# Fourfold row copies of a hybrid decoder step: from TensorE matmuls and repeated transposes to transfers through DRAM

## Chip, cores and metric

The kernel runs on one core of one Trainium2 chip. The metric is the device time of one launch in microseconds (us). The kernel before took 2336.71 us (median of 3 runs, 2336.39 to 2338.29). The profiled execution, from which all durations are read, took 2337.24 us; its instructions span 2335.5 us, so 1.7 us lie around the span.

## What is computed

One layer of a hybrid decoder is applied to a prompt of 256 tokens and to a sample group of 8 sequences with 8 new tokens each, 320 token columns in all. Cut to what matters here:

```python
# mLSTM, 4 heads, dk 256, dv 512 (per sequence)
C_new = decay * C + sum_s w_end[s] * k[s] (x) v[s]      # 8 sample states of 256 x 512 per head
# HGRN2, 8 heads, dk 128, dv 256
S_new = exp(G_end) * S + sum_s (k[s] * exp(G_end - G[s])) (x) i[s]   # 8 sample states of 128 x 256 per head
# around them: x @ w_in, sigmoid merge of two branch projections, w_out, LayerNorm,
# relu(x1 @ w_up)^2 @ w_down, LayerNorm
```

The change touches how the outer products for the sample's states get their operands. Each sequence has only 8 tokens, and the products must keep float32 accuracy although the matmuls run in a reduced format (float32r). Every operand is therefore split into a rounded part "hi" and a rest "lo", and a product is hi·hi + hi·lo + lo·hi (+ lo·lo). With a sequence's 8 tokens repeated four times on 32 partitions, keys as (hi, lo, hi, lo) and values as (hi, hi, lo, lo), one matmul over 32 partitions sums all four products at once.

## The kernel before

**Main stream.** The weights are cut into 304 tiles of 2048 rows x 128 columns, each in two units of 1024 rows. A unit is loaded into one of three raw buffers (`wr`), rounded by ACT to `hi` (line 467) and subtracted by DVE to `lo` (line 469); as soon as a raw buffer is free, its next load is issued on SP's queue (`reload`, line 476). `run_main` (line 480) then issues, for each of 16 steps of a tile, three matmuls of 128x320 (lines 504 to 506): 4864 steps and 14592 main matmuls in all. Everything else is side work that is woven in between.

**Who sets the order.** All engines run a fixed order that a planner (`Sched`, line 133) writes down while the kernel is built. Side work is written as generators that ask for an engine with a cost (`("pe", 400, ...)`), wait for events (`wait`), or take and give back a buffer (`acq`, `rel`). The planner keeps a planned clock per engine and issues a side instruction when its planned ready time has come: 140 ns are added from engine to engine (`LAT`) and 450 ns more before TensorE (`PE_LAT`). A DMA is taken to occupy SP for 620 ns, and a fixed allowance is added for its landing (2500 to 4500 ns, by the place in the code). The chip then runs each engine's instructions in that order. Where the allowance is too short, the instruction that needs the data waits in its engine's order, and all that stands behind it on that engine waits too.

**mLSTM heads** (about 87 us each; lines 776 to 1181). `m_V` transposes the values (`PE_T`, line 887), splits them (lines 890, 891), and for the sample multiplies the split rows `vs` by a 0/1 matrix `spread` (line 900, two matmuls of 128x512) to get the fourfold copies `vst`, which ACT evicts (line 901). `m_KW` weights the keys, and for each of two column halves `stack` (line 905) writes the fourfold split keys side by side in a staging tile; four transposes (line 960) turn them, and ACT evicts them to `kst` (line 963). `m_update` (line 1159) runs four matmuls over 32 partitions, four times a head, DVE adds the old state, and `m_store` sends it to DRAM. It waits for the events `KS` and `vst` (line 1162). `m_states` loads the old states, 16 of 256 KB a head.

**HGRN2 heads** (about 50 us each; lines 1184 to 1543). `h_i` transposes and splits the values and spreads them with two matmuls of 128x256 (line 1365) and an eviction (line 1366); `h_state` stacks the keys (line 1404), makes two transposes (line 1406) and an eviction (line 1408). `h_update` (line 1434) runs eight matmuls over 32 partitions once both are there.

**Afterwards** only the main stream is left: merge projections, output projection, the feed-forward part, and the prompt's states at the very end.

Of the kernel before, what the change touches and what calls it, by code (L numbers as in the profile page):

```python
# [8 lines left out]
F32 = mybir.dt.float32  # L9
# [67 lines left out]
def constants():  # L77
    c = np.zeros((128, C_END), np.float32)
    i = np.arange(128)
    c[:, C_ID:C_ID + 128] = i[:, None] == i[None, :]  # L80
    c[:, C_TRI:C_TRI + 128] = i[:, None] <= i[None, :]

    s = np.arange(64)
    t = s.reshape(2, 4, 8).transpose(1, 0, 2).reshape(64)
    c[64:, C_BM:C_BM + 64] = (s[:, None] <= t[None, :]) & (s[:, None] // 8 == t[None, :] // 8)
    for r in range(4):
        c[r, C_SEL + r] = c[r + 8, C_SEL + r] = 1.0
        c[r + 4, C_SEL + 4 + r] = c[r + 12, C_SEL + 4 + r] = 1.0
    start = np.zeros(TOK, bool)
    start[0] = True  # L90
    start[NP_::NT] = True
    c[:4, C_SC:C_SC + TOK] = ~start
    c[:4, C_SC + TOK:C_SC + 2 * TOK] = np.where(start, -1e38, 0.0)
    m = np.zeros((128, len(LEVELS), 64), np.int32)
    for n, b in enumerate(LEVELS):
        right = (i // b) % 2 == 1
        t = i[right]
        m[:, n, :] = (i[:, None] // (2 * b) == t[None, :] // (2 * b)) & ((i[:, None] // b) % 2 == 0)

    r = np.zeros((2, 64, 2, 4, 4, 8), np.float32)  # L100
    for b in range(NB):
        for n in range(4):
            for i in range(8):
                r[1 - n // 2, 8 * b + i, b // 4, b % 4, n, i] = 1.0
    return c, m.reshape(128, -1), r.reshape(128, 256)

# [144 lines left out]
def pe_r(n):  # L251
    return max(108.0, n * 0.425)
# [31 lines left out]
class Program:  # L284
# [48 lines left out]
    def carve(self):  # L333
# [20 lines left out]
        self.bc = Pool([B(712) for _ in range(2)])  # L354
        self.eb0 = B(512)
        self.eb = Pool([self.eb0])
        self.stg = Pool([B(256) for _ in range(2)])
        self.qn0 = B(256)
        self.qn = Pool([self.qn0])
        X = Part(self.rx)  # L360
# [17 lines left out]
        self.ktk = Pool([A.three(2, 128)])  # L378
        self.it2 = [B.three(3, 256) for _ in range(2)]
        self.it = Pool(self.it2)  # L380
        self.hstg = Pool([B(256) for _ in range(2)])
# [19 lines left out]
    def carve_h(self):  # L401
        C = self.Part(self.pool.tile([128, 5120], F32, name="f3h", tag="f3"))
        qz = C(256)
        self.hqz = Pool([qz])
        pp = C(512)
        self.pp = Pool([pp])
        for x in (qz, self.ats0, pp[:, 480:512], *(y[64:128, 2, :] for y in self.it2)):
# [181 lines left out]
    def start(self):  # L589
# [25 lines left out]
        self.dma(self.f2[:, 448:704], d["spread"])  # L615
        self.spread = self.ra[:, 6400:6656].rearrange("p (g n) -> p g n", g=2)
        nc.gpsimd.tensor_copy(self.lmask, lm)
        nc.gpsimd.tensor_copy(self.spread, self.f2[:, 448:704].rearrange("p (g n) -> p g n", g=2))
# [254 lines left out]
    def m_V(self, h):  # L873
# [18 lines left out]
            yield rel(self.sbank, b)  # L892
        yield rel(self.vr, vr)
        yield post(m["Vt"])

        vst = yield acq(self.vst)
        m["vst_"] = vst
        for g in range(2):
            b = yield acq(self.sbank)
            yield ("pe", pe_r(512), lambda: self.mm(b, self.spread[:, g, :], vs, start=True, stop=True))  # L900
            yield ("act", act(512, True), lambda: self.A(vst[:, g, :], b))
            yield rel(self.sbank, b)
        yield post(m["vst"])

    def stack(self, st, src, his):

        v = self.nc.vector
        w = st.rearrange("p (b r t) -> p b r t", r=4, t=8)
        x = src.rearrange("p (b t) -> p b t", t=8).unsqueeze(2).to_broadcast([128, 8, 2, 8])
        step = his[1] - his[0]  # L910
        los = [r for r in range(4) if r not in his]
        pick = lambda rs: w[:, :, rs[0]:rs[0] + 2 * step - (step - 1):step, :]
        hi, lo = pick(his), pick(los)
        yield ("act", act(128), lambda: self.A(hi.bitcast(F32R), x))
        yield ("dve", dve(128), lambda: v.tensor_tensor(lo.bitcast(F32R), x, hi, ALU.subtract))

    def m_KW(self, h):
        nc, v, m = self.nc, self.nc.vector, self.mh[h]
# [33 lines left out]
        kst = yield acq(self.kst)  # L952
        m["kst_"] = kst
        b = yield acq(self.sbank)
        bv = b.rearrange("p (g k) -> p g k", g=2)
        for c in range(2):
            st = yield acq(self.stg)
            yield from self.stack(st, kw[:, c, 256:320], (0, 2))
            for g in range(2):
                yield ("pe", PE_T, lambda: nc.tensor.transpose(bv[:, g, 128 * c:128 * c + 128], st[:, 128 * g:128 * g + 128], self.ident))  # L960
            yield rel(self.stg, st)
        yield rel(self.kw, kw)
        yield ("act", act(512, True), lambda: self.A(kst, bv))
        yield rel(self.sbank, b)
        yield post(m["KS"])

    def ln_post(self, h, i, src, den, hb, parts, psum):

# [215 lines left out]
    def h_start(self, h):  # L1184
# [5 lines left out]
        for n in ("f", "q", "lv", "o", "pre8", "suf", "I", "SP", "S", "aT", "qz", "ist", "sdone", "got", "ld"):  # L1190
            m[n] = Ev()
        m["i"] = [Ev(), Ev()]
        m["Y"] = [Ev() for _ in range(9)]
# [142 lines left out]
    def h_i(self, h):  # L1336
# [25 lines left out]
        b = yield acq(self.sbank)  # L1362
        bv = b.rearrange("p (g k) -> p g k", g=2)
        for g in range(2):
            yield ("pe", pe_r(256), lambda: self.mm(bv[:, g, :], self.spread[:, g, :], vst[:, 0, :], start=True, stop=True))
        yield ("act", act(512, True), lambda: self.A(vst, bv))
        yield rel(self.sbank, b)
        yield post(m["ist"])

    def h_load(self, h):  # L1370

# [13 lines left out]
    def h_state(self, h):  # L1385
# [13 lines left out]
        ks = fs[:, 0, 256:320]  # L1399
        yield ("dve", dve(64), lambda: v.tensor_tensor(ks, qk[:, 0, 256:320], ks, ALU.mult))  # L1400
        kst = yield acq(self.hkst)
        b = yield acq(self.sbank)
        st = yield acq(self.hstg)
        yield from self.stack(st, ks, (0, 2))
        for g in range(2):
            yield ("pe", PE_T, lambda: nc.tensor.transpose(b[:, 128 * g:128 * g + 128], st[:, 128 * g:128 * g + 128], self.ident))  # L1406
        yield rel(self.hstg, st)
        yield ("act", act(256, True), lambda: self.A(kst, b[:, 0:256].rearrange("p (g k) -> p g k", g=2)))
        yield rel(self.sbank, b)
        ob = yield acq(self.sbank)  # L1410
        m["ob2"] = ob
        yield wait(m["ld"])
# [21 lines left out]
    def h_update(self, h, kst, sm, e):  # L1434

        v, m = self.nc.vector, self.hh[h]
        yield wait(m["ist"])
        vst = m["vst"]
        ps = yield acq(self.sbank, 4)
        yield ("pe", PE_4 + 2 * pe_r(256), lambda: [self.mm(  # L1440
# [384 lines left out]
    def run(self, pool):  # L1825
# [8 lines left out]
        self.vx, self.kx, self.main_end = Pool([]), Pool([]), Ev()  # L1834
        self.sD = [self.dr.tile([128, 768], F32, name=f"sD{j}") for j in range(HH)]
        self.kD = [self.dr.tile([128, 2, 2, 256], F32, name=f"kD{j}") for j in range(MH)]
        self.vD = [self.dr.tile([128, 2, 2, 512], F32, name=f"vD{j}") for j in range(MH)]
        self.ln = [dict(c=Ev(), end=Ev(), pre=Ev(), m=Ev(), fin=Ev(), s=[Ev() for _ in range(KT)]) for _ in range(2)]
        self.xq, self.xq_ev = [None] * KT, [Ev() for _ in range(KT)]
# [5 lines left out]

INS = dict(
    xT=(128, KT, TOK), wif=(128, KT, 8), wt=(len(UNITS), 128, 1024), vec=(128, V_END), m0=(MH, NB), n0=(128, 64),
    C0=(MH, NB, 128, 1024), S0=(HH, 128, NB, HV), cst=(128, C_END), lmask=(128, len(LEVELS) * 64), spread=(128, 256),
)
OUTS = dict(  # L1850
    y=(128, KT, TOK), Cp=(MH, 128, 2, DV), n_out=(128, 72), m_out=(MH, 9), Sp=(HH, 128, HV),
# [10 lines left out]
def lay_out(x_prompt, x_sample, state_mlstm_C, state_mlstm_n, state_mlstm_m, state_hgrn_S, hg_lb_logits, w_in,  # L1862
# [11 lines left out]
    cst, lmask, spread = constants()  # L1874
    pad = np.zeros((124, 1), np.float32)
    col = lambda a: np.concatenate([f(a).reshape(MH, 1), pad], 0)
    vec = np.concatenate([part(ml_norm_g), part(hg_norm_g), part(ln1_g), part(ln1_b), part(ln2_g), part(ln2_b),
# [7 lines left out]
        S0=f(state_hgrn_S)[0].transpose(1, 2, 0, 3), cst=cst, lmask=lmask, spread=spread)  # L1885


def take_out(r):
# [31 lines left out]
```

## Time and profile before

| what | value |
|---|---|
| median of 3 runs | 2336.71 us (2336.39 to 2338.29) |
| profiled execution, its span | 2337.24 us, 2335.5 us |
| TensorE (PE) busy | 2320.3 us, 99% of the span |
| VectorE (DVE), ScalarE (ACT) busy | 1370.3 us (59%), 1049.6 us (45%) |
| DMA: bytes, mean rate | 425 MB, 182 GB/s |
| DMA share, 70 to 435 us (mLSTM heads) | 0.62 to 0.74 |
| DMA share, 500 to 862 us (HGRN2 heads) | 0.54 |

How to read it: PE is busy nearly without a break, and the profile's chain of waits stays on it. A matmul's modelled duration (about 310 ns for 128x320) overlaps with its neighbours', so what one matmul costs is read from the distance between starts: 147 ns in the main stream. The last side matmul of the heads (line 1518) starts at 862.3 us. The times in the timeline are counted from the span's start.

### The profile page before, as it was taken

Reading aid. Unit: us, or ns where it says so; the run is one execution under the profiler, and the core shown is the slowest. Engines: PE = TensorE matmul, PEld = TensorE weight load, DVE = VectorE, ACT = ScalarE, POOL = GpSimd, SP = SyncE. Lnnn points to the kernel's source line nnn. Section 1 sums busy time; section 2 is a strip of 40 time slices with the busy share of each in tenths; the row PEclk is TensorE's granted clock in tenths of the full one; section 3 lists DMA queues with packets and bytes.
Section 4 is the critical chain, followed back from the end, with each engine's and each line's share of the span. In section 5 each row is a group of like instructions: output and inputs, shape, how many; then the busy total and the mean of one; then the engine's idle time right before and its main releaser. Section 6 shows DMA issues by size and latency. Waiting matters only on the chain.

```text
span 2335.5 us, 39111 instructions
## 1 busy us (share of the span) xinstructions
PE 2320.3 (99%) x15858; PEld 2274.2 (97%) x15858; DVE 1370.3 (59%) x2320; ACT 1049.6 (45%) x1669; POOL 13.4 (1%) x57
## 2 busy tenths in 40 slices
PE   8999999999999999999999999999999999999998
PEld 7999999999999999999999999999999999999998
DVE  5566557666766776555555767544554455445555
ACT  4444445455555465444433446532443344334434
POOL 0000000000000000000000000000000000000000
PEclk9999999999999999999999999999999999999999
DMA  5777776555555554554555644444444444444465
GB/s 207 258 269 265 256 237 227 196 183 181 181 181 175 183 195 166 181 173 170 176 171 176 221 167 142 147 153 145 149 149 151 148 147 152 150 148 146 153 226 180
DMA packets 143564, 425.03 MB, mean 182 GB/s; under 512 B 16404, under 2 KB 37780, under 8 KB 142360
## 3 DMA queue, kind: packets, MB, share of 16 engines
q1 hardware_dynamic: 142232, 416.25, 51.7%
q0 software_dynamic: 1152, 6.29, 0.8%
q8 instruction: 124, 2.03, 0.4%
q14 instruction: 56, 0.46, 0.1%
HBM read 371.57 MB, written 50.90 MB: 181 GB/s over the span
## 4 chain that ended last, share of the span: by engine, by line
PE 98%; DVE 1%; DMA 0%; ACT 0%; SPq 0%; issue 0%; DVEq 0%
PE bank L327 97%; DVE f3m L1809 0%; DVE f3m L1814 0%; DMA wr<-wt 0%; PE bank L1113 0%; PE bank L1518 0%; PE bank L887 0%; DMA f<-scr 0%; PE bank L1348 0%; SPq L330 0%; PE bank L960 0%; PE bank L1406 0%; PE bank L1353 0%; PE bank L1467 0%; PE bank L934 0%
## 5 line engine op out<-in xcount | busy, mean ns | idle before, releaser
L469 DVE TENSOR_TENSOR wl<-wr,wh 128x1024 fp32r<-128x1024 f32 (+1 forms) x430 | 525.8, 1223 | 474.2 <-ACT wh L321 468.7
L327 PE MATMUL bank<-xh,wh 128*128 128x320 f32 (+1 forms) x2432 | 793.2, 326 | 0.7 <-ACT wh L321 0.7
L327 PE MATMUL bank<-xh,wl 128*128 128x320 f32 (+1 forms) x2432 | 754.0, 310 | 0.0
L327 PE MATMUL bank<-xl,wh 128*128 128x320 f32 (+1 forms) x2432 | 752.0, 309 | 0.0
L321 ACT ACTIVATE wh<-wr 128x1024 fp32r<-128x1024 f32 (+1 forms) x430 | 453.6, 1055 | 448.0 <-PE bank L327 426.1
L327 PEld LDWEIGHTS bank<-xh,wh 128*128 128x128 f32 x2432 | 459.0, 189 | 21.1 <-issue 15.0
L327 PEld LDWEIGHTS bank<-xl,wh 128*128 128x128 f32 x2432 | 459.6, 189 | 3.7
L327 PEld LDWEIGHTS bank<-xh,wl 128*128 128x128 f32 x2432 | 458.4, 188 | 0.2 <-DVE wl L469 0.2
L469 DVE TENSOR_TENSOR bb<-wr,bb 128x1024 fp32r<-128x1024 f32 x179 | 219.3, 1225 | 234.6 <-ACT bb L321 234.5
L327 PE MATMUL bank<-xh,bb 128*128 128x322 f32 x1280 | 287.2, 311 | 0.0
L327 PE MATMUL bank<-ra,bb 128*128 128x320 f32 x1264 | 283.6, 309 | 0.0
L321 ACT ACTIVATE bb<-wr 128x1024 fp32r<-128x1024 f32 x179 | 188.8, 1055 | 207.5 <-PE bank L327 199.8
L327 PE MATMUL bank<-rxb,bb 128*128 128x320 f32 x1112 | 255.4, 309 | 0.0
L327 PE MATMUL bank<-ra,wh 128*128 128x320 f32 x892 | 249.9, 309 | 0.0
L327 PEld LDWEIGHTS bank<-xh,bb 128*128 128x128 f32 x1280 | 215.9, 188 | 0.0
L327 PEld LDWEIGHTS bank<-ra,bb 128*128 128x128 f32 x1264 | 210.7, 188 | 0.4
L327 PE MATMUL bank<-xl,bb 128*128 128x322 f32 x640 | 198.7, 310 | 0.0
L327 PEld LDWEIGHTS bank<-rxb,bb 128*128 128x128 f32 x1112 | 188.4, 188 | 0.2
L321 ACT ACTIVATE f<-f,misc 128x320 f32<-128x320 f32 x210 | 118.2, 563 | 149.5 <-DVE f L1777 137.1
L327 PE MATMUL bank<-rxb,wh 128*128 128x320 f32 x596 | 184.2, 309 | 0.0
L327 PE MATMUL bank<-rxb,wl 128*128 128x320 f32 x596 | 183.8, 308 | 0.0
L327 PEld LDWEIGHTS bank<-ra,wh 128*128 128x128 f32 x892 | 161.5, 188 | 1.1 <-DVE ra L1548 0.9
(257 smaller groups left out, 2230.6 us busy)
## 6 DMA issues: line engine op xcount, KB each, us to landing
wr<-wt SPq DMA_DIRECT2D x607, 512.0 KB, 3.3
rx<-C SPq DMA_DIRECT2D x34, 256.0 KB, 5.7
Cs<-rx SPq DMA_DIRECT2D x34, 256.0 KB, 5.0
f<-C SPq DMA_DIRECT2D x30, 256.0 KB, 4.9
Cs<-f SPq DMA_DIRECT2D x30, 256.0 KB, 4.2
vD<-ra SPq DMA_DIRECT2D x4, 1024.0 KB, 7.1
f<-S SPq DMA_DIRECT2D x8, 512.0 KB, 6.1
f3h<-S SPq DMA_DIRECT2D x8, 512.0 KB, 5.7
```

The costliest lines, as they stand in the source:

```text
L321: return self.nc.scalar.activation(out, in_, func, **kw)
L327: self.nc.tensor.matmul(*a, **kw)
L469: self.V().tensor_tensor(lo[:, c], raw[:, c], hi[:, c].bitcast(F32), ALU.subtract)
```

## The change

Fourfold copies are no longer made on TensorE. `vs` (hi on partitions 64 to 127, lo on 0 to 63) is written four times to a DRAM tile whose rows are ordered sequence, copy, token; hi rows go to two of the copies and lo rows to the other two. One transfer then reads the tile back as two groups of 128 rows. The keys are transposed once, unsplit (two transposes a head instead of four; one instead of two for HGRN2), split into hi and lo straight from PSUM into halves of `kst`, and then copied in the same way over the same tile. So each of the 12 heads issues 2 x 5 more transfers on SP's queue. The matrix `spread`, its load and its copy are gone. The event that a head's update waits for is set 3000 ns after the planned issue of the read.

```diff
@@ m_V @@
-        for g in range(2):
-            b = yield acq(self.sbank)
-            yield ("pe", pe_r(512), lambda: self.mm(b, self.spread[:, g, :], vs, start=True, stop=True))
-            yield ("act", act(512, True), lambda: self.A(vst[:, g, :], b))
-            yield rel(self.sbank, b)
-        yield post(m["vst"])
-
-    def stack(self, st, src, his):
...
+        yield from self.copies(vs[64:128], vs[0:64], self.vsD[h], (0, 1), vst, m["vst"])
+
+    def copies(self, hi, lo, to, his, st, ev):
+
+        w = to.rearrange("(b r t) k -> r b t k", r=4, t=8)
+        for r in range(4):
+            t = yield ("sp", 620, lambda: self.dma(w[r], (hi if r in his else lo).bitcast(F32)))
+        t = yield ("sp", 620, lambda: self.dma(st.bitcast(F32), to.rearrange("(g p) k -> p g k", g=2)), (t + 2500.0,))
+        ev.t = t + 3000.0
@@ m_KW @@
         for c in range(2):
-            st = yield acq(self.stg)
-            yield from self.stack(st, kw[:, c, 256:320], (0, 2))
-            for g in range(2):
-                yield ("pe", PE_T, lambda: nc.tensor.transpose(bv[:, g, 128 * c:128 * c + 128], st[:, 128 * g:128 * g + 128], self.ident))
-            yield rel(self.stg, st)
+            yield ("pe", PE_T, lambda: nc.tensor.transpose(b[:, 128 * c:128 * c + 128], kw[:, c, 192:320], self.ident))
         yield rel(self.kw, kw)
-        yield ("act", act(512, True), lambda: self.A(kst, bv))
+        hi, lo = kst[64:128, 0, :], kst[0:64, 0, :]
+        yield ("act", act(256, True), lambda: self.A(hi, b[64:128, 0:256]))
+        yield ("dve", dve(256, True), lambda: v.tensor_tensor(lo, b[64:128, 0:256], hi.bitcast(F32), ALU.subtract))
         yield rel(self.sbank, b)
-        yield post(m["KS"])
+        yield from self.copies(hi, lo, self.ksD[h], (0, 2), kst, m["KS"])
@@ h_i @@
-        for g in range(2):
-            yield ("pe", pe_r(256), lambda: self.mm(bv[:, g, :], self.spread[:, g, :], vst[:, 0, :], start=True, stop=True))
-        yield ("act", act(512, True), lambda: self.A(vst, bv))
...
+        yield from self.copies(hi, lo, self.vsDh[h], (0, 1), vst, m["ist"])
@@ h_state @@
-        yield from self.stack(st, ks, (0, 2))
-        for g in range(2):
-            yield ("pe", PE_T, lambda: nc.tensor.transpose(b[:, 128 * g:128 * g + 128], st[:, 128 * g:128 * g + 128], self.ident))
+        yield ("pe", PE_T, lambda: nc.tensor.transpose(b[:, 0:128], st, self.ident))
         yield rel(self.hstg, st)
-        yield ("act", act(256, True), lambda: self.A(kst, b[:, 0:256].rearrange("p (g k) -> p g k", g=2)))
+        hi, lo = kst[64:128, 0, :], kst[0:64, 0, :]
+        yield ("act", act(128, True), lambda: self.A(hi, b[64:128, 0:128]))
+        t = yield ("dve", dve(128, True), lambda: v.tensor_tensor(lo, b[64:128, 0:128], hi.bitcast(F32), ALU.subtract))
         yield rel(self.sbank, b)
+        self.s.spawn(self.copies(hi, lo, self.ksDh[h], (0, 2), kst, m["kst"]), 4, t)
@@ h_update @@
-        yield wait(m["ist"])
+        yield wait(m["ist"], m["kst"])
```

More of the change, by code (lines that the diff above doesn't have):

```diff
@@ L98, in constants @@
         m[:, n, :] = (i[:, None] // (2 * b) == t[None, :] // (2 * b)) & ((i[:, None] // b) % 2 == 0)
[L100 to L105, printed above, removed]
+    return c, m.reshape(128, -1)
 V_MLG, V_HGG, V_G1, V_B1, V_G2, V_B2, V_LB, V_BI, V_BF, V_END = 0, 16, 32, 48, 64, 80, 96, 112, 113, 114
@@ L356, in carve @@
         self.eb = Pool([self.eb0])
-        self.stg = Pool([B(256) for _ in range(2)])
         self.qn0 = B(256)
@@ L380, in carve @@
         self.it = Pool(self.it2)
-        self.hstg = Pool([B(256) for _ in range(2)])
+        self.hstg0 = [B(128) for _ in range(2)]
+        self.hstg = Pool(self.hstg0)
         self.on0 = B.three(3, 256)
@@ L406, in carve_h @@
         self.pp = Pool([pp])
-        for x in (qz, self.ats0, pp[:, 480:512], *(y[64:128, 2, :] for y in self.it2)):
+        for x in (qz, self.ats0, *(x[:, 0:64] for x in self.hstg0), pp[:, 480:512], *(y[64:128, 2, :] for y in self.it2)):
             self.nc.gpsimd.memset(x, 0.0)
@@ L614, in start @@
         self.dma(lm, d["lmask"])
-        self.dma(self.f2[:, 448:704], d["spread"])
-        self.spread = self.ra[:, 6400:6656].rearrange("p (g n) -> p g n", g=2)
         nc.gpsimd.tensor_copy(self.lmask, lm)
-        nc.gpsimd.tensor_copy(self.spread, self.f2[:, 448:704].rearrange("p (g n) -> p g n", g=2))
         nc.gpsimd.memset(self.ones_r.bitcast(F32), 1.0)
@@ L897, in m_V @@
         m["vst_"] = vst
-        for g in range(2):
-            b = yield acq(self.sbank)
-            yield ("pe", pe_r(512), lambda: self.mm(b, self.spread[:, g, :], vs, start=True, stop=True))
-            yield ("act", act(512, True), lambda: self.A(vst[:, g, :], b))
-            yield rel(self.sbank, b)
-        yield post(m["vst"])
-    def stack(self, st, src, his):
[L907 to L915, printed above, removed]
+        yield from self.copies(vs[64:128], vs[0:64], self.vsD[h], (0, 1), vst, m["vst"])
[5 more added lines that the diff above has]
+        ev.t = t + 3000.0
     def m_KW(self, h):
@@ L954, in m_KW @@
         b = yield acq(self.sbank)
-        bv = b.rearrange("p (g k) -> p g k", g=2)
         for c in range(2):
-            st = yield acq(self.stg)
-            yield from self.stack(st, kw[:, c, 256:320], (0, 2))
-            for g in range(2):
-                yield ("pe", PE_T, lambda: nc.tensor.transpose(bv[:, g, 128 * c:128 * c + 128], st[:, 128 * g:128 * g + 128], self.ident))
-            yield rel(self.stg, st)
+            yield ("pe", PE_T, lambda: nc.tensor.transpose(b[:, 128 * c:128 * c + 128], kw[:, c, 192:320], self.ident))
         yield rel(self.kw, kw)
-        yield ("act", act(512, True), lambda: self.A(kst, bv))
+        hi, lo = kst[64:128, 0, :], kst[0:64, 0, :]
+        yield ("act", act(256, True), lambda: self.A(hi, b[64:128, 0:256]))
+        yield ("dve", dve(256, True), lambda: v.tensor_tensor(lo, b[64:128, 0:256], hi.bitcast(F32), ALU.subtract))
         yield rel(self.sbank, b)
-        yield post(m["KS"])
+        yield from self.copies(hi, lo, self.ksD[h], (0, 2), kst, m["KS"])
     def ln_post(self, h, i, src, den, hb, parts, psum):
@@ L1189, in h_start @@
         m["qk"], m["fs"], m["iv"] = a.three(2, 384), a.three(2, 320), a.three(2, 320)
-        for n in ("f", "q", "lv", "o", "pre8", "suf", "I", "SP", "S", "aT", "qz", "ist", "sdone", "got", "ld"):
+        for n in ("kst", "f", "q", "lv", "o", "pre8", "suf", "I", "SP", "S", "aT", "qz", "ist", "sdone", "got", "ld"):
             m[n] = Ev()
@@ L1361, in h_i @@
         yield post(m["I"])
-        b = yield acq(self.sbank)
-        bv = b.rearrange("p (g k) -> p g k", g=2)
-        for g in range(2):
-            yield ("pe", pe_r(256), lambda: self.mm(bv[:, g, :], self.spread[:, g, :], vst[:, 0, :], start=True, stop=True))
-        yield ("act", act(512, True), lambda: self.A(vst, bv))
-        yield rel(self.sbank, b)
-        yield post(m["ist"])
+        yield from self.copies(hi, lo, self.vsDh[h], (0, 1), vst, m["ist"])
     def h_load(self, h):
@@ L1398, in h_state @@
         yield ("dve", 80, lambda: v.tensor_copy(sm[:, 0:8], sv(fs[:, 1, :])[:, :, 7]))
-        ks = fs[:, 0, 256:320]
-        yield ("dve", dve(64), lambda: v.tensor_tensor(ks, qk[:, 0, 256:320], ks, ALU.mult))
+        st = yield acq(self.hstg)
+        yield ("dve", dve(64), lambda: v.tensor_tensor(st[:, 64:128], qk[:, 0, 256:320], fs[:, 0, 256:320], ALU.mult))
         kst = yield acq(self.hkst)
         b = yield acq(self.sbank)
-        st = yield acq(self.hstg)
-        yield from self.stack(st, ks, (0, 2))
-        for g in range(2):
-            yield ("pe", PE_T, lambda: nc.tensor.transpose(b[:, 128 * g:128 * g + 128], st[:, 128 * g:128 * g + 128], self.ident))
+        yield ("pe", PE_T, lambda: nc.tensor.transpose(b[:, 0:128], st, self.ident))
         yield rel(self.hstg, st)
-        yield ("act", act(256, True), lambda: self.A(kst, b[:, 0:256].rearrange("p (g k) -> p g k", g=2)))
+        hi, lo = kst[64:128, 0, :], kst[0:64, 0, :]
+        yield ("act", act(128, True), lambda: self.A(hi, b[64:128, 0:128]))
+        t = yield ("dve", dve(128, True), lambda: v.tensor_tensor(lo, b[64:128, 0:128], hi.bitcast(F32), ALU.subtract))
         yield rel(self.sbank, b)
+        self.s.spawn(self.copies(hi, lo, self.ksDh[h], (0, 2), kst, m["kst"]), 4, t)
         ob = yield acq(self.sbank)
@@ L1836, in run @@
         self.kD = [self.dr.tile([128, 2, 2, 256], F32, name=f"kD{j}") for j in range(MH)]
+        rows = lambda name, n, k: [self.dr.tile([32 * NB, k], F32, name=f"{name}{j}") for j in range(n)]
+        self.ksD, self.vsD, self.ksDh, self.vsDh = rows("ksD", MH, DK), rows("vsD", MH, DV), rows("ksDh", HH, HK), rows("vsDh", HH, HV)
         self.vD = [self.dr.tile([128, 2, 2, 512], F32, name=f"vD{j}") for j in range(MH)]
@@ L1847 @@
     xT=(128, KT, TOK), wif=(128, KT, 8), wt=(len(UNITS), 128, 1024), vec=(128, V_END), m0=(MH, NB), n0=(128, 64),
-    C0=(MH, NB, 128, 1024), S0=(HH, 128, NB, HV), cst=(128, C_END), lmask=(128, len(LEVELS) * 64), spread=(128, 256),
+    C0=(MH, NB, 128, 1024), S0=(HH, 128, NB, HV), cst=(128, C_END), lmask=(128, len(LEVELS) * 64),
 )
@@ L1873, in lay_out @@
         wt[n] = w[name][r:r + 1024, c:c + 128].reshape(8, 128, 128).transpose(1, 0, 2).reshape(128, 1024)
-    cst, lmask, spread = constants()
+    cst, lmask = constants()
     pad = np.zeros((124, 1), np.float32)
@@ L1884, in lay_out @@
         C0=f(state_mlstm_C)[0].reshape(NB, MH, 2, 128, DV).transpose(1, 0, 3, 2, 4).reshape(MH, NB, 128, 1024),
-        S0=f(state_hgrn_S)[0].transpose(1, 2, 0, 3), cst=cst, lmask=lmask, spread=spread)
+        S0=f(state_hgrn_S)[0].transpose(1, 2, 0, 3), cst=cst, lmask=lmask)
 def take_out(r):
```

## The prediction

> **What bounds the kernel now.** I read the page's busy table first, then the chain of waits, then who PE waited for.
>
> ```profile
> PE 2320.3 (99%) x15858; PEld 2274.2 (97%) x15858; DVE 1370.3 (59%) x2320; ACT 1049.6 (45%) x1669; POOL 13.4 (1%) x57
> PE 98%; DVE 1%; DMA 0%; ACT 0%; SPq 0%; issue 0%; DVEq 0%
> ```
>
> ```profile
> PE bank L327 <- ACT wh L321: 0.7, 1, 0.7
> PE bank L327 <- DVE ra L891: 0.5, 1, 0.5
> ```
>
> PE sets the end. The second fence is from the waits of PE (us in total, times, longest). Three more such waits, 7.3 us, lie in the first 11 us; after that PE waits 0.5 us once, and never for a DMA. So a matmul that goes is worth its distance between starts, and any new wait on PE is paid in full. The forecast is a race between these two.
>
> **What goes from PE.** In the built order of the changed kernel PE has 40 matmuls fewer: 8 spreads of 128x512, 16 of 128x256 and 16 transposes. Prices are from PE's timeline (start, duration), one main matmul before and one behind:
>
> ```profile
> 238.81 0.31 PE L327 MATMUL bank<-xh,wl 128*128 128x320 f32 x1
> 238.96 0.40 PE L327 MATMUL bank<-ra 128*128 128x512 f32 x1
> 239.20 0.30 PE L327 MATMUL bank<-xh,wh 128*128 128x320 f32 x1
> ...
> 451.90 0.31 PE L327 MATMUL bank<-xh,wl 128*128 128x320 f32 x1
> 452.05 0.28 PE L327 MATMUL bank<-rh,ra 128*128 128x256 f32 x1
> 452.17 0.31 PE L327 MATMUL bank<-xh,wh 128*128 128x320 f32 x1
> ...
> 226.65 0.31 PE L327 MATMUL bank<-xh,wl 128*128 128x320 f32 x1
> 226.80 0.27 PE L887 MATMUL bank<-cst,f 128*128 128x128 f32 x1
> 226.83 0.39 PE L327 MATMUL bank<-xh,wh 128*128 128x320 f32 x1
> 227.06 0.31 PE L327 MATMUL bank<-xl,wh 128*128 128x320 f32 x1
> ```
>
> A main matmul takes 0.147 us to the next start. From 238.81 to 239.20 are 0.39, so a 128x512 spread costs 0.24; 451.90 to 452.17 gives 0.12 for 128x256. A transpose also slows the matmul behind it: 226.65 to 227.06 is 0.41, less 2 x 0.147 is 0.12. Sum: 8 x 0.24 + 16 x 0.12 + 16 x 0.12 = 5.8 us. Head 0's first spread also waited for line 891: it started 0.80 us after the matmul before it (65.87 to 66.67), 0.65 over 0.147, and that wait goes with it. In place of it nothing on PE needs line 891 at that point. **PE gains 6.4 us** (5.8 if that wait moves to another matmul).
>
> **What costs nothing.** ACT loses evictions of 0.5 to 0.6 us and gains shorter ones, DVE loses 16 stacking subtractions of 0.29 us and gains 12 of at most 0.69 us (the row of line 891); both change by less than 10 us beside 1000 and more idle, and PE waited for DVE 0.5 us in all. SP issues 120 transfers more and one load (`spread`) less; at 0.33 to 0.46 us an issue (its timeline) that is some 50 us of a queue that waits 844 us for line 469 alone. Behind them stand weight loads: one issued at 151.03 was split from 157.9 and first used at 164.1, 13 us against a landing of at most 7.2, so a delay of 5 us is covered; beyond that PE would wait for weights. POOL's removed copy and the removed load are in the first 20 us, where PE waits for the split of x: 0 to -0.4 us, taken as 0. PE gets some ten more semaphore waits; the nearest row is PEld's idle "issue" time, 23.6 us in 74 cases, 0.32 each, so 0 to 3.2 us; taken as 0, since waits on that engine for loads already stand in the old order beside matmuls at 0.147.
>
> **What moves.** The updates come later: the first ones of heads 0 to 3 go from steps 144, 300, 460, 620 to 160, 307, 469, 629, those of the HGRN2 heads come 9 to 19 steps later; the last head matmul stays at step 1597 in both orders, so nothing is pushed behind the main stream.
>
> **What is added on the way to PE.** Each of the 12 heads now has two gates: SP must wait until four writes have landed before it issues the read, and the update on PE must wait for the read. By the code the read stands 620 + 2500 + 140 = 3.26 us behind the last write's issue, and the update at least 620 + 3000 + 140 + 450 = 4.21 us behind the read's. In the built order the later read (keys, mostly) has just this: 4.2 to 4.5 us in the mLSTM heads, 4.2 to 4.8 in the others. Behind a late update stands the whole main stream. The trace of before has no such copy; its nearest rows are DMA issues with their median landing, in 66 to 435 us and then in 435 to 862 us:
>
> ```profile
> wr<-wt SPq DMA_DIRECT2D x86, 512.0 KB, 4.3
> rx<-C SPq DMA_DIRECT2D x32, 256.0 KB, 5.3
> vD<-ra SPq DMA_DIRECT2D x4, 1024.0 KB, 7.1
> hT<-f SPq DMA_DIRECT2D x16, 160.0 KB, 4.9
> ```
>
> ```profile
> wr<-wt SPq DMA_DIRECT2D x100, 512.0 KB, 3.4
> f<-S SPq DMA_DIRECT2D x6, 512.0 KB, 6.1
> oT<-f SPq DMA_DIRECT2D x15, 160.0 KB, 2.9
> sD<-f SPq DMA_DIRECT2D x8, 128.0 KB, 4.3
> ```
>
> In the second stretch (HGRN2 heads) small stores land in 2.9 and whole 512 KB weights in 3.4 us, under 3.26 and 4.21: seven HGRN2 heads cost nothing. Upper bound by sD: (4.3 - 3.26) x 7 = 7 us. HGRN2 head 0 has two S loads right ahead of its reads (6.1 us for the second against 4.8): 0 to 1.3, I take 0.5.
> In the mLSTM stretch stores land in 4.9 and 256 KB loads in 5.3 us, but these medians come from bursts of states. Upper bound a head: (4.9 - 3.26) + (5.3 - 4.21) = 2.7. Lower bound 0, if the read finds the queue empty. For heads 0, 2 and 3 the key writes start 5 to 7 us behind vD (1 MB, 7.1 us), when the queue is just emptying: I take 1.0 each.
> Head 1 is worse: in its order kD, vD, two C loads and two weights stand between and ahead of the value writes.
>
> ```profile
> 160.98 0.46 SPq L330 DMA_DIRECT2D vD<-ra  x1
> 162.93 0.33 SPq L330 DMA_DIRECT2D wr<-wt  x1
> ```
>
> That weight load landed after 7.2 us. A 128 KB write in its place, some 1 us quicker, lands in 6: the read of the values is 2.8 late, and the last key write stands behind it on SP. That write, 1.2 over its allowance (the mean of 4.9 and 4.0, gaD's median in the later stretch, is 4.5), and a read of about 4.7 add 1.2 + 0.5: 4.5 in all; 1 to 7 by the rows.
> **New waits: 3 x 1.0 + 4.5 + 0.5 = 8.0 us** (1 to 23). The C load with the least spare was issued at 179.98, landed in 5.2 us and was used at 185.55, 0.4 us later; the changed order has it no tighter, so 0, up to 1 a head.
>
> **Clock.** At the start the matmuls of 128x320 stood 0.27 us apart from 10.79 to 13.46, and 0.147 behind that, after gaps of up to 3.3 us: 10 x 0.12 = 1.2 us lost. A new wait as long could cost that again: 0 to 1.2 for each one over 3 us, taken as 0 since no gap in mid-stream is there to read. [...]
>
> **Sum.** 2337.24 - 6.4 + 8.0 = 2338.8 for the profiled execution, which stood 0.5 above the median of the runs: **2338.3 us**, +0.07%. This kernel's measurement can tell about 0.2%, 4.7 us.
>
> **Rivals.**
> 1. *Forecast: the new waits eat the gain*, 5 to 11 us of them within 0.2%: 0.50.
> 2. *The transfers are hidden.* For it: packets are small, 1.5 MB a head at most beside 150 to 260 GB/s, and 3.26 and 4.21 us exceed the quiet rows. Against it: 0.74 of the DMA time is taken in the mLSTM stretch. With waits of 1: 2336.7 - 6.4 + 1 = 2331.3, faster: 0.16.
> 3. *Slower: the writes queue.* Place: the four value and four key writes of the mLSTM heads. If the writes take the DMA queues longer than their bytes say, the backlog behind vD has not gone when the key writes come, and every mLSTM head pays like head 1: 4 x 4.5 = 18, 2336.7 - 6.4 + 18 = 2348.3. It decides from 11 us of waits on. For it: vD, kD and weights keep landing in 7 us there; against it: a lone weight load behind them was back to 4.8 us (166.99). 0.34.
> [...]
>
> **Range.** Low end: waits of nearly nothing, 2331.5. High end: the time of rival 3, 2348.
>
> **What would show it.** On PE's waits, a row of the update's matmuls with a DMA as releaser: near 8 us in 12 cases or fewer, most of it at head 1 (right); nothing (rival 2); over 11, in all mLSTM heads (rival 3). On SP's waits, a read waiting for its writes' landing. Starts 0.27 apart behind a wait tell of the clock. I would be wrong as a whole if PE waits for weights, or if ACT or DVE become its releasers.

## The result and the profile after

The changed kernel takes 2362.09 us (median of 4 runs, 2362.05 to 2365.45) against 2337.39 of the kernel before in the same comparison: ratio 1.0108, 95% interval 1.0096 to 1.0120, slower by 25 us. The forecast was 2338.3 with 2331.5 to 2348.0, so the time lies outside its range. The profiled execution took 2362.11 us, 24.87 more than that of before.

The busy table and the chain of waits of the page after:

```profile
PE 2323.4 (98%) x15818; PEld 2276.6 (96%) x15818; DVE 1369.5 (58%) x2316; ACT 1036.6 (44%) x1637; POOL 13.2 (1%) x58
...
PE 94%; DMA 3%; DVE 1%; ACT 1%; issue 0%; SPq 0%; DVEq 0%; ACTq 0%
PE bank L321 93%; DMA wr<-wt 1%; DMA ksD<-ra 1%; DMA ra<-ksD 0%; DMA vsD<-ra 0%; ACT wh L315 0%; SPq L324 0%; DVE f3m L1781 0%; DVE f3m L1786 0%; DMA ra<-ksDh 0%; PE bank L1490 0%; PE bank L878 0%; PE bank L1091 0%; DVE wl L463 0%; PE bank L1326 0%
```

PE has its 40 matmuls fewer, but the chain now runs outside PE for 6% of the span, not 2%, and the DMAs of the copies (`ksD`, `vsD`) are on it. (The chain follows back what released PE, also while PE was still busy, so the 6% are not PE's idle time.) Who PE waited for (us in total, times, longest):

```profile
PE bank L321 <- DMA ra<-ksD: 19.8, 4, 10.2
PE bank L321 <- DVE ra L661: 4.3, 1, 4.3
PE bank L321 <- DVE f L1615: 2.0, 1, 2.0
PE bank L321 <- ACT xh L315: 1.5, 1, 1.5
PE bank L321 <- DMA ra<-ksDh: 1.4, 1, 1.4
```

The first row is the four mLSTM updates, each waiting for the read of its keys; the row `ra<-ksDh` is HGRN2 head 0. The rows of L661 and `xh` lie in the first 11 us, as before. The row of L1615 is one wait of the first LayerNorm's mean at 1340 us. Before and behind the wait of head 1 the timeline of PE shows this (start, duration, idle before and its releaser):

```profile
175.27 0.31 PE L321 MATMUL bank<-xh,wl 128*128 128x320 f32 x1
185.80 0.80 PE L321 MATMUL bank<-ra 32*128 32x512 f32 x4 [10.22 <-DMA ra<-ksD]
...
187.23 0.47 PE L321 MATMUL bank<-xh,wl 128*128 128x320 f32 x1
187.50 0.47 PE L321 MATMUL bank<-xh,wh 128*128 128x320 f32 x1
...
192.04 0.31 PE L321 MATMUL bank<-xl,wh 128*128 128x320 f32 x1
192.19 0.31 PE L321 MATMUL bank<-xh,wl 128*128 128x320 f32 x1
```

The wait has a tail: until 191.8 the matmuls start 0.27 us apart, and only then 0.15 again. Two stretches of that place, with the granted clock behind the busy times of the engines, then the DMA share and GB/s:

```profile
core 0: us, PE busy (x) PEld busy (x) DVE busy (x) ACT busy (x) POOL busy (x), PEclk, DMA share, GB/s
155.00:175.00 20.00, 20.00 (x142) 18.21 (x141) 9.33 (x19) 7.84 (x14) 0.00 (x0) 1.00 0.95 328
175.00:190.00 15.00, 4.78 (x21) 4.10 (x21) 4.16 (x7) 2.95 (x5) 0.00 (x0) 0.61 0.77 253
```

Behind the wait half the clock is granted (0.50 from 185.80 to 191.85 us; 0.61 is the mean of a stretch at half and at full clock), and in the 20 us ahead of this wait the DMA engines are 95% busy, at 328 GB/s.

**Where the 24.9 us come from.** PE's gaps ahead of five updates (last main matmul to update, less 0.15) are 1.1, 10.4, 4.0, 4.9 us (heads 0 to 3) and 1.6 (HGRN2 head 0): 22.1. Behind four of them PE then works at half clock for 6.05, 3.41, 4.11 and 3.41 us; at 0.267 a matmul and not 0.147, 45% of that is lost: 7.6. The LayerNorm wait costs 2.3 (main matmuls counted from the two traces). That is 32.0. The kernel is only 24.9 slower, so 7.1 were gained; the matmuls that went are what is left to explain them.

**Why the updates waited** is read from SP's timeline, here around head 1 (start, duration of the issue):

```profile
164.08 0.39 SPq L324 DMA_DIRECT2D kD<-ra  x1
164.56 0.60 SPq L324 DMA_DIRECT2D f<-C  x1
165.22 1.83 SPq L324 DMA_DIRECT2D vsD<-ra  x1
167.10 1.53 SPq L324 DMA_DIRECT2D vD<-ra  x1
...
170.83 1.70 SPq L324 DMA_DIRECT2D vsD<-ra  x1
...
178.24 0.38 SPq L324 DMA_DIRECT2D ra<-vsD  x1
178.67 0.57 SPq L324 DMA_DIRECT2D ksD<-ra  x1
...
182.89 0.38 SPq L324 DMA_DIRECT2D ra<-ksD  x1
```

PE stood at the update from 175.42 on. The last key write was not even issued then; it came at 178.67, right behind the read of the values, which had waited on SP for its own writes. With the least allowances of the prediction (3.26 from last write to read, 4.21 from read to update, 7.47 together) each wait can be taken apart:

| mLSTM head | last key write later than 7.47 us ahead of PE | write to read, over 3.26 | read to update, over 4.21 | wait |
|---|---|---|---|---|
| 0 | -1.0 | +3.5 | -1.4 | 1.1 |
| 1 | +10.7 | +1.0 | -1.3 | 10.4 |
| 2 | +3.8 | +1.6 | -1.4 | 4.0 |
| 3 | +4.0 | +2.3 | -1.4 | 4.9 |

The reads landed sooner than allowed. The writes landed later. But the large term in heads 1 to 3 is the first: SP issued the key writes late, measured against PE's arrival. PE did not come early: by the planner's own clocks head 1's last key write is due at 164.1 us and its update at 171.8; on the chip they stood at 178.7 and 175.4. Both are late, SP by far more. SP's waits are not all for the copies: from 140 to 180 us it waited 10.4 us for the stores of C states (`Cs<-rx`), much as in the kernel before (10.5 for `Cs<-rx` and `Cs<-f`). No run takes that part away.

### The profile page after: what moved, and what is told of

Its sections match the earlier page's. It is cut to its first block, busy times and chain, and to the rows that moved or that the text cites. A ratio compares the mean times of both kernels' runs of the same rounds, so it can differ in the third digit from the quotient of the medians.

```text
span 2360.3 us, 39191 instructions
## 1 busy us (share of the span) xinstructions
PE 2323.4 (98%) x15818; PEld 2276.6 (96%) x15818; DVE 1369.5 (58%) x2316; ACT 1036.6 (44%) x1637; POOL 13.2 (1%) x58
## 4 chain that ended last, share of the span: by engine, by line
PE 94%; DMA 3%; DVE 1%; ACT 1%; issue 0%; SPq 0%; DVEq 0%; ACTq 0%
PE bank L321 93%; DMA wr<-wt 1%; DMA ksD<-ra 1%; DMA ra<-ksD 0%; DMA vsD<-ra 0%; ACT wh L315 0%; SPq L324 0%; DVE f3m L1781 0%; DVE f3m L1786 0%; DMA ra<-ksDh 0%; PE bank L1490 0%; PE bank L878 0%; PE bank L1091 0%; DVE wl L463 0%; PE bank L1326 0%
```

## Experiments

The theory at the start (A) was rival 3 put down to the spread of a write's rows in the DRAM tile, 8 x 8: such a write would take the DMA queues longer than its bytes say. No trace had shown that; it was the author's assumption. It is tested first. The row that the expectation speaks of is that of the four key waits of PE (`ra<-ksD`, 19.8 us in the changed kernel). All ratios are to the kernel before, with 95% intervals.

### Rows as 16 x 4

```diff
-        w = to.rearrange("(b r t) k -> r b t k", r=4, t=8)
+        w = to.rearrange("(b h r t) k -> r (b h) t k", h=2, r=4, t=4)
```

> Edit: the rows of each DRAM tile are ordered sequence, half, copy, token of the half, so a write has 16 x 4 rows as its outer sizes and not 8 x 8; the built order of every engine is that of the changed kernel, instruction for instruction. [...] Rival B (the allowances are too short for any write there; the spread does not matter): the row stays at 18 to 21 us and the time within 3 us of 2362.

Measured: 2360.34 us, 1.0099 (1.0084 to 1.0114); 1.8 less than the changed kernel, and the two intervals overlap. The key waits of PE are 17.3 us. Theory A falls: time and waits hardly moved. Rival B's time came, and its waits nearly (18 to 21 were expected). Yet the row order does show in the packet counts of the two pages, first the changed kernel, then this one:

```profile
DMA packets 156862, 437.50 MB, mean 185 GB/s; under 512 B 17540, under 2 KB 49028, under 8 KB 155656
```

```profile
DMA packets 157630, 437.50 MB, mean 186 GB/s; under 512 B 18308, under 2 KB 49796, under 8 KB 156424
```

The kernel before had 16404 packets under 512 B. The change adds 96 writes and 24 reads, drops one load and brings 1136 such packets; the rows as 16 x 4 bring 768 more at the same bytes, which is eight for each write. Over how many DMA engines a write ran, the pages do not show. They were not what cost the time: with more of them the run took 1.8 us less. This run also shows each landing (issues, KB, median us; the later rows are the HGRN2 heads):

```profile
vsD<-ra SPq DMA_DIRECT2D x16, 128.0 KB, 5.2
ra<-vsD SPq DMA_DIRECT2D x4, 512.0 KB, 5.2
...
vsDh<-rh SPq DMA_DIRECT2D x32, 64.0 KB, 2.1
...
ksD<-ra SPq DMA_DIRECT2D x16, 64.0 KB, 6.1
ra<-ksD SPq DMA_DIRECT2D x4, 256.0 KB, 2.9
ksDh<-ra SPq DMA_DIRECT2D x32, 32.0 KB, 3.2
```

A 64 KB write needs 6.1 us in the mLSTM stretch, where the DMA engines of this run are 75% busy on the average and up to 96%, and 2.1 in the HGRN2 stretch, at 61%: equal bytes, but other neighbours.

### Updates later

```diff
-        t = yield ("sp", 620, lambda: self.dma(st.bitcast(F32), to.rearrange("(g p) k -> p g k", g=2)), (t + 2500.0,))
-        ev.t = t + 3000.0
+        t = yield ("sp", 620, lambda: self.dma(st.bitcast(F32), to.rearrange("(g p) k -> p g k", g=2)), (t + 6000.0,))
+        ev.t = t + 9000.0
```

> Edit: in copies the read stands 6000 ns (not 2500) behind the last write and the event 9000 ns (not 3000) behind the read; the planner puts the updates later by 10 us a copy, the writes stay as they are. If the loss is only that PE arrives at the updates too early (theories A and B alike): PE waits for a DMA under 2 us, the granted clock stays at 1.0, and the time is the 2336.7 of before less the 6.4 of matmuls that went, 2330 to 2334. Rival C (SP stands in order before the read, and what is behind it, weights and states, comes late): SP still waits for the writes, PE now waits for weights or for C, and the time is over 2345. If the 2.3 us lost at 1340 us (the LayerNorm mean waiting for DVE) is the order's doing, it may go or stay: 2332 or 2334.5.

Measured: 2334.31 us, 0.9987 (0.9977 to 0.9996). That is 0.3 above the expected range. Waits for the copies are down to 0.7 us, waits for C are 1.0, and the clock is full up to the last 2.2 us. The loss is one of timing: PE came to the updates before the copies were there. But the edit also moves the reads on SP, behind the key writes in heads 1 to 3; a later run parts the two.

### Both together

> Both edits together. Theory A: the spread only sets the landing, and with late updates the landing is covered, so the same as the run with late updates alone within 0.1% (2330 to 2334). [...]

Measured: 2332.92 us, 0.9983 (0.9973 to 0.9992); 1.4 us less than with late updates alone, which is 0.06% and inside both intervals. With late updates the row order makes no difference that these runs can tell.

### Only the HGRN2 heads

`m_V`, `m_KW`, `stack` and the matrix `spread` stay as in the kernel before; only the HGRN2 part of the diff is taken:

```diff
@@ h_i @@
...
-        for g in range(2):
-            yield ("pe", pe_r(256), lambda: self.mm(bv[:, g, :], self.spread[:, g, :], vst[:, 0, :], start=True, stop=True))
...
+        yield from self.copies(hi, lo, self.vsDh[h], (0, 1), vst, m["ist"])
@@ h_state @@
-        yield from self.stack(st, ks, (0, 2))
...
+        self.s.spawn(self.copies(hi, lo, self.ksDh[h], (0, 2), kst, m["kst"]), 4, t)
```

> Edit: only the HGRN2 heads' copies go through DRAM; the mLSTM heads are those of the kernel before. Removed on PE: 16 spreads of 128x256 and 8 transposes at 0.12 us, 2.9 us. If the HGRN2 heads pay only at the first of them, as in the profile of the changed kernel (a gap of 1.75 us and 3.4 us at half clock, 3.3 us together): 2337, within 0.1% of before. If its loss there comes from the backlog of the mLSTM heads and goes with it: 2333.5 to 2334.5. If the 2.3 us lost at 1340 us belongs to this part's order: 2.3 more in either case.

Measured: 2336.52 us, 0.9995 (0.9985 to 1.0004). PE waits 0.2 us for `ksDh`. From 800 to 1600 main steps the same matmuls come 2.5 us earlier than before, near the 2.9 of the sum; the LayerNorm wait (1.7 us here) takes most of it back. So the change costs nothing in the HGRN2 heads as such, and the wait at HGRN2 head 0 (1.6 us in the changed kernel) hangs on the mLSTM heads ahead of it.

### Another queue

```diff
-            t = yield ("sp", 620, lambda: self.dma(w[r], (hi if r in his else lo).bitcast(F32)))
+            t = yield ("pool", 620, lambda: self.nc.gpsimd.dma_start(w[r], (hi if r in his else lo).bitcast(F32)))
```

The read goes the same way.

> After the first four runs theory A has fallen (16 x 4 rows instead of 8 x 8: 2360.3, hardly better). What is left: F (place in the queue): between 150 and 180 us the DMA runs at 0.9 and more of its time, 350 to 440 GB/s, with kD, vD, states and weights issued ahead on SP's queue, and the writes land behind them in 4 to 8 us. G (bandwidth or engine load as such): any transfer is that slow there, from whatever queue. Edit: the writes and reads of copies are issued by POOL on its own queue; allowances, row order and the updates' places stay (within a few steps). F: the copies pass SP's backlog, writes land in 2 to 4 us, PE's waits for the copies come to under 8 us in all, the time is 2334 to 2343. G: the waits stay at 15 us or more and the time is over 2352. If POOL's issue (0.53 us a row in the kernel before) and landing are slower by themselves, the HGRN2 heads will wait too.

Measured: 2361.02 us, 1.0105 (1.0087 to 1.0122). G's time came, and PE's waits for copies are 16.8 us in all, as G has it; but more than half of them stand in the HGRN2 heads. PE's waits (first fence) and the landings from 66 to 435 us (second):

```profile
PE bank L321 <- DMA ra<-ksD: 7.7, 4, 5.2
PE bank L321 <- DMA ra<-ksDh: 6.6, 2, 4.8
...
PE bank L321 <- DVE f L1055: 3.2, 1, 3.2
PE bank L321 <- DMA rh<-vsDh: 2.5, 1, 2.5
```

```profile
vsD<-ra POOLq DMA_DIRECT2D x15, 128.0 KB, 5.9
ksD<-ra POOLq DMA_DIRECT2D x16, 64.0 KB, 5.2
```

The writes land no sooner than from SP (5.9 and 5.2 against 5.2 and 6.1; the latter are of the run with rows as 16 x 4, since the changed kernel's page has no landings), so they pass nothing: G, for the landing. The mLSTM waits fall all the same, 19.8 to 7.7, where the copies have left SP's order. In turn the HGRN2 heads pay 9.1 us: on POOL the writes and reads of the two copies stand behind each other's waits (at 465.6 us the read of the values has waited 3.0 us for the key writes).

### kD and vD behind the copies

```diff
-        yield wait(m["KH"], m["Vt"])
+        yield wait(m["KH"], m["Vt"], m["KS"], m["vst"])
```

> Edit: m_CP waits for the planned events of both copies before it issues kD (512 KB) and vD (1 MB), so these 1.5 MB a head stand behind the copies on SP's queue and not ahead of or among them; nothing else is asked for. F with kD and vD as the main backlog: 1.5 MB at about 350 GB/s are 4.4 us less ahead of the key copies, so the waits of heads 0 to 3 fall by about 4 each, to 5 or less together (head 1 perhaps 5 alone), and the time is 2336 to 2344. F with the states and weights as the backlog, kD and vD not decisive: the waits stay over 15 us, the time over 2352.

Measured: 2352.62 us, 1.0060 (1.0043 to 1.0077), 9.5 less than the changed kernel. The waits are between the two views, the time at the edge of the second:

```profile
PE bank L321 <- DMA ra<-ksD: 8.3, 3, 5.0
...
PE bank L321 <- DMA f<-C: 3.1, 2, 2.4
```

The key waits fell by 11.5 us; 3.1 come back as waits for the next C states, behind which half clock follows once (from 114.47 us). These delay PE, and a PE that comes later waits less: it reaches head 1's update at 179.91 and not at 175.42, while the last key write is out only 2.3 us sooner. So at head 1 most of the drop is a wait that was paid earlier. In heads 2 and 3 PE came sooner than in the changed kernel, and still the first term of the table fell to 0.8 and 0.6. So kD and vD are a part of the backlog, not all of it, and moving them has its own price.

### Two writes instead of four

```diff
-        w = to.rearrange("(b r t) k -> r b t k", r=4, t=8)
-        for r in range(4):
-            t = yield ("sp", 620, lambda: self.dma(w[r], (hi if r in his else lo).bitcast(F32)))
+        w = to.rearrange("(b t r) k -> (b t) r k", r=4, t=8)
+        step = his[1] - his[0]
+        los = [r for r in range(4) if r not in his]
+        for src, rs in ((hi, his), (lo, los)):
+            x = src.bitcast(F32).unsqueeze(1).to_broadcast([64, 2, to.shape[1]])
+            t = yield ("sp", 620, lambda: self.dma(w[:, rs[0]:rs[0] + 2 * step - (step - 1):step, :], x))
```

> Edit: two writes a copy instead of four, each of the same 64 partitions, with every row written to its two copies (row order sequence, token, copy); the bytes stay, 48 issues go, and the read comes earlier by two issues. H (the number of transfers: SP's issue time stretched to 1.3 to 1.8 us there, each transfer waiting for a place among those in flight): the waits halve, the time is 2343 to 2352. F or G (bytes ahead decide): within 5 us of 2362, since the updates' places move earlier with the reads.

Measured: 2356.08 us, 1.0080 (1.0065 to 1.0095), 6.0 less than the changed kernel. The waits are 17.4 us in four, the longest 5.9 and not 10.2. Neither H (halved) nor F (no gain) in full. In the profiled execution, the slowest of the four (2358.32), head 1 waits 4.5 us less, heads 2 and 3 wait 0.9 and 1.1 more, and HGRN2 head 0 does not wait. The edit changes the packets too: from 66 to 435 us 4275 are under 512 B, about the 4271 of the changed kernel, with half as many writes.

### The values' read behind the key writes

```diff
@@ copies; m_V passes gate=m["kw"], m_KW passes mark=m["kw"] @@
...
+        if mark:
+            mark.t = t
+        t += 2500.0
+        if gate:
+            yield wait(gate)
+            t = max(t, gate.t)
...
```

> Edit: in the mLSTM heads the read of the values is issued only behind the four key writes, so that its wait for the value writes no longer holds the key writes; allowances, row order and the updates' places (steps 160, 306, 469, 629) are those of the changed kernel. J: the last key write of head 1 comes 2.4 us earlier (the wait ahead of the read at 178.24 there), those of heads 2 and 3 by about as much (their reads stood 5.6 and 5.6 us behind the last value write, against 3.26 allowed); the waits of PE on the four heads fall from 19.8 by 6 to 9, and the time is 2350 to 2356. F (bytes ahead) alone: the key writes come earlier but land no earlier, and the time stays within 4 us of 2362.

Measured: 2353.14 us, 1.0066 (1.0051 to 1.0081), 9.0 less than the changed kernel, key waits 13.5 us in three: J. Not all of the gain is J's: the LayerNorm wait (2.3 us in the changed kernel) is absent from this profile. SP's timeline at head 1:

```profile
172.16 1.21 SPq L324 DMA_DIRECT2D ksD<-ra  x2
174.54 0.38 SPq L324 DMA_DIRECT2D ra<-vsD  x1
177.62 0.38 SPq L324 DMA_DIRECT2D ra<-ksD  x1
```

PE came to this update at 173.37; the last key write is out at 172.8, 0.6 ahead of that, where it was 3.3 behind it. By the same working as in the table the first term is 6.9, 1.6 and 1.8 us in heads 1 to 3, down by 3.8, 2.2 and 2.3. Hardly more than one instruction a head has another place. The second term stays at 1.6 to 2.7 in these heads: the landing is late for itself.

### The event late, the read not

```diff
-        ev.t = t + 3000.0
+        ev.t = t + 12500.0
```

> Edit: the read keeps its 2500 ns behind the last write, only the event moves, to 12500 ns behind the read; together the same 15000 as in the run with both later. J (SP in order: a read that waits for its writes holds the key writes, the weights and the states behind it, and that alone costs PE): SP waits 10 us or more for the writes, PE waits for the copies, weights or C, the time is over 2340. F without that (only PE's arrival counts): the same as the run with both later, 2331 to 2336.

Measured: 2335.09 us, 0.9988 (0.9979 to 0.9998), the same as with both later. So the place of the event is enough: the loss goes with the time at which PE comes, and not with the place of the reads. In heads 2 and 3 the values' read still stands ahead of the last key write, and PE does not wait there (its list has no wait for a copy): a read that held SP was harmless here, where nothing on PE was due. (In head 1 the new order has it behind the key writes.)

### The three orders together

> Edit: the read of the values behind the key writes, kD and vD behind the copies, and two writes a copy instead of four, all three together, with the allowances of the changed kernel. If their gains (9.5 us for kD and vD, 6.0 for two writes, and that of the run before) are of different causes and add up: 2338 to 2346. If they are one and the same backlog, met three ways: about the best of them, 2350 or more. If moving kD and vD makes PE wait for the next head's C, as it did alone (3.1 us), that stays.

Measured: 2342.49 us, 1.0024 (1.0015 to 1.0033). The gains of the three runs (9.5, 6.0, 9.0) would add up to 24.5; 19.6 came. So they add up for the larger part, and are not one backlog met three ways. Left are 3.7 us for `ksD`, 1.8 for `vsDh`, 1.7 for C, 1.4 for DVE.

### The best of both

The two edits above together: two writes a copy, and the allowances of 6000 and 9000 ns.

> Edit: two writes a copy and the late allowances (6000 and 9000 ns): the candidate that is to beat both kernels. Waits for copies gone, clock at 1.0 throughout, PE's 40 matmuls fewer: 2330.3 for everything gained (2336.7 less 6.4), 2331 to 2333.5 expected, since the runs with late updates kept 1.2 to 2 us of waits.

Measured: 2332.95 us, 0.9982 (0.9973 to 0.9991): faster than both kernels, by 0.18% and 1.2%. From the run with late updates and four writes (2334.31) it cannot be told: the intervals overlap. No wait for a copy is left in PE's list:

```profile
PE bank L321 <- DVE ra L661: 4.3, 1, 4.3
PE bank L321 <- ACT xh L315: 2.1, 1, 2.1
PE bank L321 <- DVE f L1618: 1.5, 1, 1.5
PE bank L321 <- ACT wh L315: 0.7, 1, 0.7
PE bank L321 <- DVE xl L656: 0.3, 1, 0.3
```

At main step 1600 it is 5.9 us ahead of before; the LayerNorm wait (L1618 in this file) takes 1.8 back.

### The clock alone

The kernel before gets 30 pairs of small matmuls in the feed-forward stage; the second of each pair waits for `k` clears on POOL, with `k` from 5 to 26:

```diff
...
+            yield ("pe", 212, lambda: self.mm(b[:, 0:128], self.ones, self.ones, start=True, stop=True))
+            for _ in range(k):
+                yield ("pool", 0, lambda: self.nc.gpsimd.memset(self.ones, 1.0))
+            yield ("pe", 212, lambda: self.mm(b[:, 0:128], self.ones, self.ones, start=True, stop=True))
...
```

> The kernel before, with 30 PE waits put into the feed-forward stage, 20 us apart, each on 5 to 26 clears of the table of ones on POOL (the values stay the same), for gaps of about 1 to 6 us. If the clock halves only after an idle stretch of 3.4 us: no half clock behind gaps under 3.4 us, always behind longer ones. If it is judged in fixed slots of 3.41 us, as the starts of the half-clock stretches in the changed kernel suggest (178.20, 280.60, 369.34, 488.81: whole multiples of 3.413 apart): gaps of 1.7 to 3.4 us do it where over about 1.6 us of them fall into one slot, gaps under 1.6 never, and each half-clock stretch is 3.41 us or a multiple.

Measured, in one profile of 2488.07 us: 30 gaps of 0.8 to 6.4 us, from start to start. None up to 1.9 us brought half clock; of 2.4 us two in three did, of 2.9 us all three, of 3.5 us two in three; from 4.0 us on all. Two gaps, each with the stretch behind it:

```profile
core 0: us, PE busy (x) PEld busy (x) DVE busy (x) ACT busy (x) POOL busy (x), PEclk, DMA share, GB/s
1735.90:1738.30 2.40, 0.32 (x3) 0.05 (x1) 1.34 (x2) 1.03 (x2) 1.85 (x10) 1.00 0.54 198
1738.86:1742.27 3.41, 3.41 (x15) 3.41 (x14) 0.31 (x1) 1.03 (x2) 0.00 (x0) 0.50 0.44 154
1784.70:1788.10 3.40, 0.30 (x3) 0.04 (x1) 1.63 (x2) 1.48 (x3) 2.65 (x14) 1.00 0.33 104
1788.10:1791.60 3.50, 3.44 (x23) 3.44 (x24) 0.00 (x0) 0.24 (x2) 0.01 (x1) 1.00 0.32 126
```

The gap of 2.4 us was followed by a half clock of 3.41 us, and the one of 3.5 us by none. So it is not the length alone. Fixed slots of 3.413 us, the step that the starts in the changed kernel give (102.40 us for 30 slots from 178.20 to 280.60), explain it: the first gap lies in the slot from 1735.45 to 1738.86, the second is cut by a boundary at 1786.65. All 19 half-clock stretches of this stage start on that grid and last one or two slots. That is the second view of the expectation.

## Why the prediction was wrong, step by step

- **"PE gains 6.4 us"**: right, as far as the account goes. 7.1 are left in that of the changed kernel, 5.9 in the best version.
- **"What costs nothing"**: right for ACT, DVE and the weights, which are no new releasers on PE. Wrong for SP: its issues were priced at 0.33 to 0.46 us, and took up to 1.83 around head 1. The delay was checked against the weights alone, which stood it, and not against the copies' own place on SP.
- **The landing against the allowances**: the write term was right at head 1 (over 3.26 by 1.0; 1.2 taken) and too small elsewhere (3.5, 1.6 and 2.3 in heads 0, 2 and 3; upper bound 1.6), the read term too high (2.8 to 2.9 us from read to update against 4.7 taken).
- **"For heads 0, 2 and 3 ... I take 1.0 each", "4.5 in all" for head 1**: this is the step that failed. It gave the key writes their planned place on SP, but for 2.8 us at head 1, and counted only the landing behind them. The place itself slipped by 10.7, 3.8 and 4.0 us. Measured: 1.1, 10.4, 4.0 and 4.9; heads 1 to 3 are even above the upper bounds (7 and 2.7), which left the slip out. Three edits that take something off SP's queue ahead of the key writes each make up for a part of the time: the values' read behind the key writes (9.0 us), kD and vD behind the copies (9.5), half the number of writes (6.0). These are times of the whole kernel, with the LayerNorm wait in the first and a later PE in the second, and not sizes of the slip. What makes up the rest of it stays open; SP's waits for the C states' stores are one candidate that no run takes away.
- **HGRN2 heads**: 0 for seven of them is right; head 0 took 1.6 and not 0.5, and half clock behind it.
- **"Clock ... taken as 0"**: wrong, 7.6 us. It was priced at 1.2 a gap; 1.5 to 2.7 came, four times, one of them behind a wait of 1.6 us.
- **Rivals**: rival 3 had the direction and, with 18 us of waits, nearly the size (22.1). That the sizes are near is in part luck: its ground, that every head pays like head 1, is wrong (1.1 to 10.4). A backlog with vD in it is borne out in part (kD and vD behind the copies). Rows as 16 x 4 make 1.8 us, inside the intervals, so the order of the rows is no ground for it either.
- **Not in any case**: the 2.3 us of the LayerNorm. The order on PE there is that of before, and the wait is 0 to 2.0 us across the variants; ahead of it ACT waits for a weight load that lands late (2.41 us in the changed kernel). Why it lands late so often is left open.

Left open too: whether an issue of 1.8 us on SP is a full queue. The halved number of writes helped, but it also made the writes larger and the read earlier.

## What to carry to other kernels

Before a transfer replaces work of the bottleneck engine, count not only how long it takes to land but when its queue will get to it: here a read that waited for its own writes held the issues behind it on SP (2.4 us ahead of 178.24 in head 1), and in heads 1 to 3 the slip of the place was about 2 to 11 times that of the writes' landing. This bounce through DRAM ran better behind no large store (9.5 us less with kD and vD behind it) and with fewer, larger writes (6.0 us less with two instead of four), and its consumer needed the slack of the busy stretch, not that of a quiet one (15 us planned from last write to use were enough and 5.5 were not; nothing between was tried). Price a stall of the matmul engine with its tail at half clock: 7.6 us here, on top of 22.1 us of waits.

## What the runs showed of the hardware

- Half clock came and went in fixed slots of 3.413 us: in the changed kernel the four stretches start at 178.20, 280.60, 369.34 and 488.81, whole multiples apart (30, 56 and 91 slots from the first). They last 13.65, 3.41, 6.83 and 3.41 us: 4, 1, 2 and 1 slots. The full-clock slots ahead of the four hold 2.62, 2.32, 2.01 and 1.44 us of PE idle (no matmul running, by the profile). Slots with 1.57 (at 273.77) and 1.87 us (at 1338.73) were not followed by half clock, so the idle time of a slot alone does not set a sharp limit there.
- A 64 KB write landed in 2.1 us in the quiet stretch and in 6.1 in the mLSTM stretch (medians of the run with rows as 16 x 4), 2.2 and 5.2 from POOL's queue. The gap is not fixed: in the run with rows as 16 x 4 the key writes landed in 5.7, 4.4, 7.8 and 6.5 us (medians around heads 0 to 3), and the 64 KB writes of the HGRN2 heads in 3.4 up to 520 us and 2.0 behind that.
